# Tokens past 192 of any expert in one loop at the end of the expert part, and PLE products staged in a buffer each

## The chip, the cores and the metric

One core of a Trainium2 chip runs the kernel. The metric is the device time of one execution in microseconds; lower is better. The kernel is one layer of a trunk for 2,048 tokens of width 1,024, all in float32.

## The reference, cut to what matters

The layer has a mixer part (two token mixers, merged and added to x), an expert part, and an end part. The change touches the second and its borders:

```
h = rmsnorm(x) ; top group of 4 by softmax(h @ w_grp), then the top 2 of its 8 experts
x = x + sum over the two experts e of gate[e] * ((silu(h @ w1[e]) * (h @ w3[e])) @ w2[e])
x = x + sigmoid(rmsnorm(x) @ w_pg) * (p @ w_ple)          (PLE: p has 256 columns per token)
out = rmsnorm(x)
```

There are 32 experts with w1, w3 of 1,024 x 512 and w2 of 512 x 1,024. No expert has a limit of tokens: any of them may get from 0 to 2,048, by the data. All 4,096 assignments (two per token) have to be computed.

## The kernel before, in words

**Precision.** A float32 weight is split in two reduced-precision parts, `hi` (written by ScalarE, ACT, as a copy) and `lo` (written by VectorE, DVE, as the difference), and so are the rows. TensorE (PE) then forms three products: hi by hi, lo by hi, hi by lo. In the expert part the split weights are `ehi` (L901) and `elo` (L907), the split rows `xhi` (L882) and `xlo` (L886), and the products stand in `P` (L914).

**The order of the parts.** The mixer part takes four blocks of 512 tokens, until about 1426 us. Each block's router part gives the choice of experts; the tokens are entered in a table in DRAM, and one product counts the tokens of each expert. L803 to L813 make of the counts one integer per group of 8 experts, `codes`, with three bits per expert: over 128, over 160, over 192 tokens.

**PLE products.** `ple()` (L1019 to L1028) forms p @ w_ple for blocks 1 to 3, twelve tiles of 128 tokens by 1,024 columns: PE makes two halves (L547), ACT copies each half out of PE's accumulators into a buffer `po` (L548), and the sync engine (SP) issues its store to DRAM (L1027). The buffers of `po` carry the tag `elo` and so are the five buffers (SPL = 5) in which the `elo` splits of the expert part will live. A string, FILL, sets how the last router steps (H), the loading of expert 0's weights (E) and the PLE products (F) alternate; the products left over come after the gathers of the first two experts. Block 0's product is formed in the end part, from buffers there.

**The expert part** (L1097 to L1138) goes through the 32 experts in ORDER. For each expert SP issues twelve weight loads of 512 KB each (eight at L722, four at L729) into one of two pools, and GpSimd (POOL) gathers rows of its first 192 tokens (L841). The loads of expert 1 are made to wait for the gathered rows of expert 0 (`behind_rows`). DVE transposes the rows (`X`, L856), and then the splits and products follow a string, PART, that spells out the order of the instructions of the running expert, of the one before (its second product: T, L925, transposes; G; B, L946; Y, the copy of the results and their scatter to DRAM by POOL, L848) and of the one that follows. The first 128 tokens are computed so. Tokens 129 to 160 and 161 to 192 are computed by `some(0)` and `some(1)`, which use smaller products in plain float32.

These stand in nested branches, by the bits of the expert's code: `more` (L1129, over 128) holds `some(0)`, between whose steps GAPS puts the first products of the next expert; inside it `most` (L1131, over 160) holds `some(1)`; inside that `beyond` (L1133, over 192) holds `rest()`, a loop `For_i(192, n, 128)` with n the expert's count. Where `more` is not taken, its Else does the next expert's first products (BEGIN). Branch hints (`skip`) tell an engine ahead of time how a branch will go: for `more` on all engines, for `most` and `beyond` on PE alone. The codes are loaded in a register of each of the five engines (L1067).

**The end part** has a string of its own, FIRST, then STEPS per tile of 128 tokens: load x1 (L1153) and the two expert rows of each token (`yt`, L1155), add them by the gates (L1165), transpose (L1199), split, the product with w_pg (L1214 to L1216), sigmoid, add. The split of w_pg, `pghi` and `pglo` (L1288, L1289), is made at its start, in buffers that the expert part leaves, and block 0's PLE products (L547) are formed meanwhile.

In `ple()` a staging buffer is taken, and in the experts' code a split's buffer:

```
o = xe.tile([128, 2, 512], F32R, name="po", tag="elo", bufs=SPL)
...
xe.tile([128, 2, 512], F32R, name=name, tag=name, bufs=SPL)
```

The first instructions of expert 0 (two `hi` and `lo` splits, X, x, y) are put in order by a planner together with the PLE products ahead of them (`in_order`); what follows from L1097 on has the order that the code spells out.

Of the kernel before, what the change touches and what calls it, by code (L numbers as in the profile page):

```python
# [11 lines left out]
I32 = mybir.dt.int32  # L12
# [66 lines left out]
def tile_hybrid_block(ctx: ExitStack, tc: tile.TileContext, a, out):  # L79
# [31 lines left out]
    counts = const.tile([1, NE], I32, name="counts")  # L111
    codes = const.tile([1, NG], I32, name="codes")
# [37 lines left out]
    with ExitStack() as fin, ExitStack() as route_ctx, ExitStack() as moe_ctx:  # L150
# [148 lines left out]
        def setup_route():  # L299
# [26 lines left out]
            C["bits"] = bits = mr.tile([1, 3, NE], F32, name="bits")  # L326
            for j in range(3):
                for i in range(EPG):
                    vec.memset(bits[:, j].rearrange("o (g i) -> o g i", i=EPG)[:, :, i], float(2 ** j * 8 ** i))
# [384 lines left out]
        def load_expert(i):  # L714

            e = ORDER[i]
            w13, w2 = [], []
            for t in range(4):
                raw = r13[i % 2].tile([128, 2, 2, 512], F32, name="w13r", tag="w13")
# [86 lines left out]
        vec.tensor_copy(counts, pt[0:1, 0:NE])  # L806
        code = sm.tile([1, 3, NG], F32, name="code")
        for j, top in enumerate((128.0, 160.0, 192.0)):
            bit = C["bits"][:, j]
            vec.scalar_tensor_tensor(bit, pt[0:1, 0:NE], top, bit, op0=OP.is_gt, op1=OP.mult)  # L810
            vec.tensor_reduce(code[:, j], bit.rearrange("o (g i) -> o g i", i=EPG), axis=AX.X, op=OP.add)
        vec.tensor_tensor(code[:, 0], code[:, 0], code[:, 1], op=OP.add)
        vec.tensor_tensor(codes, code[:, 0], code[:, 2], op=OP.add)  # L813
# [44 lines left out]
        class Expert:  # L858
# [120 lines left out]
            def rest(self):  # L979

                e = self.e
                n = nc.values_load(counts[0:1, e:e + 1], min_val=0, max_val=T)
                with tc.For_i(192, n, 128) as r:
                    tv = xe.tile([128, 4], I32, name="tvd", tag="tvd", bufs=1)
                    for q in range(4):
                        pool.dma_start(
                            tv[32 * q:32 * q + 32],
                            tab_d[bass.ds(r * NE, 128 * NE)].rearrange("(q i e) o -> i e (q o)", q=4, i=32)[:, e])
                    yv = xe.tile([128, 1], I32, name="yvd", tag="yvd", bufs=1)
                    for q in range(4):  # L990
                        vec.tensor_copy(yv[32 * q:32 * q + 32], tv[32 * q:32 * q + 32, q:q + 1])
                    token_rows(vec, tv, pgrp)
                    gx = xe.tile([128, 4, 256], F32, name="gx", tag="y", bufs=2)
                    vec.memset(gx, 0.0)
                    gather(gx, tv)
                    xt = xe.tile([128, KT, 128], F32, name="xt", tag="y", bufs=2)
                    turn_rows(xt, gx)
                    ph = [mm() for _ in range(2)]
                    for k in range(KT):
                        for n in range(2):  # L1000
                            pe.matmul(ph[n], xt[:, k], self.w13[k][:, n], start=k == 0, stop=k == KT - 1)
                    t = xl.tile([128, 512], F32, name="rg", tag="yz", bufs=1)
                    act.activation(t, ph[0], AF.Silu)
                    vec.tensor_tensor(t, ph[1], t, op=OP.mult)
                    pt = px()
                    for j in range(4):
                        pe.transpose(pt[:, 128 * j:128 * j + 128], t[:, 128 * j:128 * j + 128], ident)
                    vec.tensor_copy(t, pt)
                    py = [px() for _ in range(2)]
                    for k in range(4):  # L1010
                        for c in range(2):
                            pe.matmul(py[c], t[:, 128 * k:128 * k + 128], self.w2[k][:, 512 * c:512 * c + 512],
                                      start=k == 0, stop=k == 3)
                    yr = xe.tile([128, D], F32, name="yr", tag="y", bufs=2)
                    for c in range(2):
                        act.activation(yr[:, 512 * c:512 * c + 512], py[c], AF.Copy)
                    put(yr, yv)

        def ple():  # L1019
            for m4 in range(1, NB):  # L1020
                if m4 == 3:
                    ple_turn(praw, pturn[3])
                for m in range(MB):
                    o = xe.tile([128, 2, 512], F32R, name="po", tag="elo", bufs=SPL)
                    o = o.rearrange("p n c -> p (n c)").bitcast(F32)
# [70 lines left out]

        with tc.manual_schedule():  # L1097
            ex[0].keep(())
            do(ex[0], BEGIN)
            for i in range(NE + 1):  # L1100
# [13 lines left out]
                if now is None:  # L1114
                    ple_turn(praw, pT)
# [12 lines left out]
                if now:  # L1128
                    with tc.If((code & bit) != 0, preferred_fallthrough_block=True, label=f"more{i}") as more:  # L1129
                        now.some(0, gaps(then, GAPS, f"most{i}", code, 2 * bit))  # L1130
                        with tc.If((code & 2 * bit) != 0, preferred_fallthrough_block=True, label=f"most{i}"):  # L1131
                            now.some(1, gaps(None, GAPS, f"beyond{i}", code, 4 * bit))
                            with tc.If((code & 4 * bit) != 0, preferred_fallthrough_block=True, label=f"beyond{i}"):  # L1133
                                now.rest()
                    if then:
                        then.parts = begun
                        with more.Else():
                            do(then, BEGIN)  # L1138

# [198 lines left out]
```

## Time and profile before

| | us |
|---|---|
| median of 3 runs | 2441.78 |
| lowest and highest | 2434.21, 2446.19 |
| the profiled execution: its own time | 2459.05 |
| its span | 2457.3 |
| busy: PE, DVE, ACT, POOL | 2364.7, 1440.3, 1277.6, 410.2 |
| mixer part, expert part, end part | to 1426, to about 2237, to the end |

All numbers of single instructions come from the profiled execution, whose time is 17.27 us over the median; a sum made of them is a sum against 2459.05. Times in rows are us from the span's start. PE, DVE, ACT, POOL and SP are the engines; an engine's name with a q is its sequencer, which runs branches, register operations and the issue of DMAs. "idle before <- X" tells what ended an idle time. PEclk is the granted clock of PE as a share of the full one.

### The profile page before, as it was taken

The page shows a single profiled execution, that of the slowest core. Times are in us where ns is not written, and L with a number is a line of the kernel's source. Part 1 is how long each engine was busy: PE and PEld are TensorE (multiplying, and loading weights), DVE is VectorE, ACT ScalarE, POOL GpSimd, SP SyncE. Part 2 cuts the span into 40 slices and gives each one's busy share as a digit, 9 for nine tenths or more (in the row PEclk, how much of TensorE's full clock was granted, in tenths as well). Part 3 has the DMA queues.
Part 4 walks back from the last instruction along what each step waited for, and adds up shares of the span by engine and source line. Part 5 has one row for each costly group of instructions (what it writes and reads, how often), then busy time and mean ns, then how long its engine had stood idle before and what let it go on. Part 6 is the DMA issues. An engine that isn't in the chain of part 4 may idle for free. (4 is left out here: it accounts for less than half of the span.)

```text
span 2457.3 us, 38163 instructions
## 1 busy us (share of the span) xinstructions
PE 2364.7 (96%) x13676; PEld 1898.8 (77%) x13676; DVE 1440.3 (59%) x2505; ACT 1277.6 (52%) x1963; POOL 410.2 (17%) x371
## 2 busy tenths in 40 slices
PE   7999999999999999999999998989999998998998
PEld 6888898888898978898978955666666666665887
DVE  6654445763455663536653447666666666675776
ACT  5763336752346753337733345556555655565443
POOL 1000000110000100000100033434344443431000
PEclk9999999999999999999999999999999999999999
DMA  6333443234342334442343458888779879785553
GB/s 171 92 87 95 131 138 103 65 112 129 104 150 78 87 103 129 125 126 72 100 125 98 156 177 317 308 298 321 306 294 345 308 295 343 276 340 216 196 218 125
DMA packets 313097, 445.86 MB, mean 181 GB/s; under 512 B 32442, under 2 KB 231174, under 8 KB 310752
## 3 DMA queue, kind: packets, MB, share of 16 engines
q1 hardware_dynamic: 290272, 385.68, 46.2%
q0 software_dynamic: 22528, 56.46, 6.4%
q8 instruction: 157, 2.57, 0.4%
q14 instruction: 140, 1.15, 0.1%
HBM read 401.87 MB, written 51.02 MB: 184 GB/s over the span
## 5 line engine op out<-in xcount | busy, mean ns | idle before, releaser
L182 DVE TENSOR_TENSOR wlo<-wraw,whi 128x512 fp32r<-128x512 f32 x445 | 305.1, 688 | 424.4 <-ACT whi L181 396.6
L181 ACT ACTIVATE whi<-wraw 128x512 fp32r<-128x512 f32 x448 | 281.3, 628 | 521.1 <-PE pa L206 323.9
L205 PE MATMUL pa<-h,whi 128*128 128x512 f32 x1024 | 403.4, 394 | 0.0
L206 PE MATMUL pa<-h,whi 128*128 128x512 f32 x1024 | 399.9, 390 | 0.0
L207 PE MATMUL pa<-h,wlo 128*128 128x512 f32 x1024 | 399.4, 390 | 0.0
L907 DVE TENSOR_TENSOR elo<-w13r,ehi 128x1024 fp32r<-128x1024 f32 x256 | 305.6, 1215 | 32.9 <-ACT ehi L901 12.1
L841 POOL DMA_INDIRECT rows<-h_d,tokidx x192 | 256.2, 1334 | 301.3 <-DVE elo L907 107.0
L901 ACT ACTIVATE ehi<-w13r 128x1024 fp32r<-128x1024 f32 x256 | 263.2, 1053 | 52.8 <-PE pa L914 33.4
L205 PEld LDWEIGHTS pa<-h,whi 128*128 128x128 f32 x1024 | 192.4, 188 | 42.0 <-issue 0.7
L207 PEld LDWEIGHTS pa<-h,wlo 128*128 128x128 f32 x1024 | 192.3, 188 | 40.9
L206 PEld LDWEIGHTS pa<-h,whi 128*128 128x128 f32 x1024 | 192.4, 188 | 39.5
L914 PE MATMUL pa<-ehi,xhi 128*128 128x512 f32 x512 | 182.2, 437 | 7.9 <-ACT ehi L901 3.6
L914 PE MATMUL pa<-ehi,xlo 128*128 128x512 f32 x512 | 164.2, 402 | 8.2 <-DVE xlo L886 8.2
L914 PE MATMUL pa<-elo,xhi 128*128 128x512 f32 x512 | 164.0, 402 | 0.9 <-DVE elo L907 0.8
L225 PE MATMUL pa<-whi,h 128*128 128x256 f32 x512 | 146.2, 286 | 0.1
L227 PE MATMUL pa<-whi,h 128*128 128x256 f32 x512 | 145.6, 285 | 0.0
L226 PE MATMUL pa<-wlo,h 128*128 128x256 f32 x512 | 145.3, 284 | 0.0
L226 PE MATMUL pa<-wlo,hi 128*128 128x256 f32 x512 | 143.9, 281 | 0.0
L225 PE MATMUL pa<-whi,hi 128*128 128x256 f32 x512 | 143.4, 280 | 0.0
L227 PE MATMUL pa<-whi,lo 128*128 128x256 f32 x512 | 143.3, 280 | 0.0
L914 PEld LDWEIGHTS pa<-ehi,xhi 128*128 128x128 f32 x512 | 93.2, 193 | 47.5 <-issue 29.3
L914 PEld LDWEIGHTS pa<-ehi,xlo 128*128 128x128 f32 x512 | 98.3, 192 | 31.9 <-DVE xlo L886 8.6
(319 smaller groups left out, 4525.7 us busy)
## 6 DMA issues: line engine op xcount, KB each, us to landing
w13r<-in_w_dram SPq DMA_DIRECT2D x256, 512.0 KB
wraw<-in_w_in_dram SPq DMA_DIRECT2D x320, 256.0 KB
w2r<-in_w_dram SPq DMA_DIRECT2D x128, 512.0 KB
wraw<-in_w_out_dram SPq DMA_DIRECT2D x64, 256.0 KB
yt<-y_d SPq DMA_DIRECT2D x16, 1024.0 KB
xt<-in_x_dram SPq DMA_DIRECT2D x32, 256.0 KB
wraw<-in_w_up_a_dram SPq DMA_DIRECT2D x32, 256.0 KB
wraw<-in_w_up_b_dram SPq DMA_DIRECT2D x32, 256.0 KB
```

The source lines that it names most:

```text
L181: whi = act.activation(hi, raw, AF.Copy)
L182: wlo = (pool if n < POOLG else vec).tensor_tensor(lo, raw, hi.bitcast(F32), op=OP.subtract)
L205: pe.matmul(ps, hi[:, k4], xhi, start=k == 0, stop=False)
L206: pe.matmul(ps, hi[:, k4], xlo, start=False, stop=False)
L207: pe.matmul(ps, lo[:, k4], xhi, start=False, stop=k == n_k - 1)
L225: pe.matmul(o, xhi[:, s], hi[:, k2], start=st, stop=False, skip_group_check=True)
L226: pe.matmul(o, xhi[:, s], lo[:, k2], start=False, stop=False, skip_group_check=True)
L227: pe.matmul(o, xlo[:, s], hi[:, k2], start=False, stop=k == n_k - 1, skip_group_check=True)
L841: ins = pool.indirect_dma_start(out=g[:, q], out_offset=None, in_=h2_d, in_offset=bass.IndirectOffsetOnAxis(ap=idx[:, at:at + 1], axis=0), ...
L901: act.activation(t, self.raw(k), AF.Copy)
L907: vec.tensor_tensor(t, self.raw(k), hi.bitcast(F32), op=OP.subtract)
L914: pe.matmul(self.ph[n], xp[:, k], w[:, n], start=k == 0 and w is hi and xp is self.xhi, stop=k == KT - 1 and xp is self.xlo)
```

## The change

Two things are changed.

- **PLE staging.** The twelve `po` tiles take five buffers of the tag `ehi`, then five of the tag `elo`, then two of the tag `y` (the buffers of the experts' results).
- **Tokens past 192.** The innermost branch `beyond` is taken out of every `most`, with its loop and its hint. Behind the last expert stands one branch, on a new value `beyond` (is any count over 192), and in it one loop to the largest count, `top`, that goes through all 32 experts and loads each one's weights again (12 loads, in the second pool). A hint for this branch is given on all five engines in the last round of the expert loop. The codes have two bits per expert now and their row holds `top` and `beyond` as well, each loaded in a register of each engine.

The loop's body, which the diff moves, is cut here; it uses `w13` and `w2` as loaded in place of the expert's own.

```diff
--- before.py
+++ after.py
@@ -108,8 +108,7 @@
     eps = const.tile([128, 1], F32, name="eps")
     vec.memset(eps, EPS)
     gate = const.tile([128, NT, 2], F32, name="gate")
-    counts = const.tile([1, NE], I32, name="counts")
-    codes = const.tile([1, NG], I32, name="codes")
+    codes = const.tile([1, NG + 2], I32, name="codes")
     gple = const.tile([128, KT], F32, name="gple")
     pgrp = const.tile([128, 1], F32, name="pgrp")
     plowf = const.tile([128, 1], F32, name="plowf")
@@ -323,8 +322,8 @@
             vec.memset(onesb, 1.0)
             C["acc"] = acc = mr.tile([128, NE], BF16, name="acc")
             vec.memset(acc, 0.0)
-            C["bits"] = bits = mr.tile([1, 3, NE], F32, name="bits")
-            for j in range(3):
+            C["bits"] = bits = mr.tile([1, 2, NE], F32, name="bits")
+            for j in range(2):
                 for i in range(EPG):
                     vec.memset(bits[:, j].rearrange("o (g i) -> o g i", i=EPG)[:, :, i], float(2 ** j * 8 ** i))
             pidx = sm.tile([128, 1], I32, name="pidx")
@@ -712,11 +711,13 @@
                 tc.add_manual_dep(ld.ins, ins.ins.name, SYNC, reason="the rows come first")
 
         def load_expert(i):
-
-            e = ORDER[i]
+            return load_weights(ORDER[i], r13[i % 2], i)
+
+        def load_weights(e, pl, i=0):
+
             w13, w2 = [], []
             for t in range(4):
-                raw = r13[i % 2].tile([128, 2, 2, 512], F32, name="w13r", tag="w13")
+                raw = pl.tile([128, 2, 2, 512], F32, name="w13r", tag="w13")
                 for n in range(2):
                     w = (a["w1"], a["w3"])[n][0, e].rearrange("(p k) c -> p k c", k=KT)
                     ld = nc.sync.dma_start(raw[:, n], w[:, 2 * t:2 * t + 2])
@@ -803,14 +804,16 @@
             next(last)
         pt = px()
         pe.matmul(pt[:, 0:NE], C["onesb"], C["acc"], start=True, stop=True)
-        vec.tensor_copy(counts, pt[0:1, 0:NE])
-        code = sm.tile([1, 3, NG], F32, name="code")
-        for j, top in enumerate((128.0, 160.0, 192.0)):
+        code = sm.tile([1, 2, NG], F32, name="code")
+        for j, top in enumerate((128.0, 160.0)):
             bit = C["bits"][:, j]
             vec.scalar_tensor_tensor(bit, pt[0:1, 0:NE], top, bit, op0=OP.is_gt, op1=OP.mult)
             vec.tensor_reduce(code[:, j], bit.rearrange("o (g i) -> o g i", i=EPG), axis=AX.X, op=OP.add)
-        vec.tensor_tensor(code[:, 0], code[:, 0], code[:, 1], op=OP.add)
-        vec.tensor_tensor(codes, code[:, 0], code[:, 2], op=OP.add)
+        vec.tensor_tensor(codes[:, 0:NG], code[:, 0], code[:, 1], op=OP.add)
+        top = sm.tile([1, 1], F32, name="top")
+        vec.tensor_reduce(top, pt[0:1, 0:NE], axis=AX.X, op=OP.max)
+        vec.tensor_copy(codes[:, NG:NG + 1], top)
+        vec.tensor_single_scalar(codes[:, NG + 1:NG + 2], top, 192.0, op=OP.is_gt)
         mix_ctx.close()
         xe = moe_ctx.enter_context(tc.tile_pool(name="xe", bufs=1, side="right", reuse_waits="tile"))
         rw = moe_ctx.enter_context(tc.tile_pool(name="rw", bufs=1, side="right", reuse_waits="tile"))
@@ -976,53 +979,56 @@
                 act.activation(yz, pz[:, 0:256], AF.Copy)
                 put(yz, ym[s][:, self.e:self.e + 1])
 
-            def rest(self):
-
-                e = self.e
-                n = nc.values_load(counts[0:1, e:e + 1], min_val=0, max_val=T)
-                with tc.For_i(192, n, 128) as r:
...
-                    put(yr, yv)
+        def rest(e, r):
+
+            w13, w2 = list(load_weights(e, r13[1]))[-1]
+            tv = xe.tile([128, 4], I32, name="tvd", tag="tvd", bufs=1)
...
+                    pe.matmul(ph[n], xt[:, k], w13[k][:, n], start=k == 0, stop=k == KT - 1)
...
+            put(yr, yv)
 
         def ple():
+            n = 0
             for m4 in range(1, NB):
                 if m4 == 3:
                     ple_turn(praw, pturn[3])
                 for m in range(MB):
-                    o = xe.tile([128, 2, 512], F32R, name="po", tag="elo", bufs=SPL)
-                    o = o.rearrange("p n c -> p (n c)").bitcast(F32)
+                    if n < 2 * SPL:
+                        o = xe.tile([128, 2, 512], F32R, name="po", tag=("ehi", "elo")[n // SPL], bufs=SPL)
+                        o = o.rearrange("p n c -> p (n c)").bitcast(F32)
+                    else:
+                        o = xe.tile([128, D], F32, name="po", tag="y", bufs=2)
+                    n += 1
                     ple_tile(m, pturn[m4], o)
                     nc.sync.dma_start(ple_d[m4 * MB + m], o)
                     yield
@@ -1094,6 +1100,8 @@
                     skip(label, code, bit, BUSY[:1])
                 yield
 
+        top = load(codes[0:1, NG:NG + 1], T)
+        beyond = load(codes[0:1, NG + 1:NG + 2], 1)
         with tc.manual_schedule():
             ex[0].keep(())
             do(ex[0], BEGIN)
@@ -1112,6 +1120,7 @@
                 if i + 2 < NE:
                     ex[i + 2].fetch()
                 if now is None:
+                    tc.mark_branch_hint_location("beyond", beyond, engines=QUEUED + BUSY)
                     ple_turn(praw, pT)
                 for word in PART.split():
                     if word in "nm":
@@ -1129,13 +1138,16 @@
                     with tc.If((code & bit) != 0, preferred_fallthrough_block=True, label=f"more{i}") as more:
                         now.some(0, gaps(then, GAPS, f"most{i}", code, 2 * bit))
                         with tc.If((code & 2 * bit) != 0, preferred_fallthrough_block=True, label=f"most{i}"):
-                            now.some(1, gaps(None, GAPS, f"beyond{i}", code, 4 * bit))
-                            with tc.If((code & 4 * bit) != 0, preferred_fallthrough_block=True, label=f"beyond{i}"):
-                                now.rest()
+                            now.some(1, iter(()))
                     if then:
                         then.parts = begun
                         with more.Else():
                             do(then, BEGIN)
+
+            with tc.If(beyond != 0, preferred_fallthrough_block=True, label="beyond"):
+                with tc.For_i(192, top, 128) as r:
+                    for e in range(NE):
+                        rest(e, r)
 
         moe_ctx.close()
         wg_p = fin.enter_context(tc.tile_pool(name="wg_p", bufs=1, side="right", reuse_waits="tile"))
```

## Rows read from the trace of the kernel before

**Rows 1.** Busy time by stage: us from, to, length, busy us of each engine, PEclk, DMA share, GB/s.

```profile
1473.00:1486.00 13.00, 3.22 (x9) 1.83 (x8) 5.80 (x5) 1.67 (x3) 10.26 (x10) 0.72 0.96 351
1486.00:2227.00 741.00, 696.76 (x4117) 479.51 (x4115) 496.99 (x479) 436.26 (x541) 291.55 (x226) 0.98 0.83 311
2227.00:2258.00 31.00, 24.59 (x73) 13.23 (x74) 14.23 (x14) 14.37 (x21) 4.03 (x2) 0.94 0.54 204
```

**Rows 2.** Waits of PE, 1486 to 2227: us in total, times, longest us.

```profile
PE pb L925 <- ACTq L1131: 14.4, 11, 3.4
PE pb L925 <- PEq L1131: 4.2, 2, 2.2
PE pb L925 <- ACTq L1133: 3.9, 2, 3.2
```

**Rows 3.** PE in time, 1473 to 1492: start us, us, instruction, idle before it.

```profile
1484.61 1.22 PE L914 MATMUL pa<-ehi,xlo 128*128 128x512 f32 x2 [8.15 <-DVE xlo L886]
1491.29 0.62 PE L914 MATMUL pa<-ehi,xhi 128*128 128x512 f32 x2
```

**Rows 4.** ACT in time, 1430 to 1492.

```profile
1448.09 0.60 ACT L548 ACTIVATE po<-pa 128x512 f32<-128x512 f32 x1 [1.12 <-PE pa L547]
1474.17 1.05 ACT L882 ACTIVATE xhi<-xr 128x1024 fp32r<-128x1024 f32 x1
```

**Rows 5.** DVE in time, 1461 to 1492.

```profile
1482.20 1.23 DVE L907 TENSOR_TENSOR elo<-w13r,ehi 128x1024 fp32r<-128x1024 f32 x1 [2.36 <-DMA ple_d<-po]
1483.34 1.22 DVE L886 TENSOR_TENSOR xlo<-xr,xhi 128x1024 fp32r<-128x1024 f32 x1
1484.47 1.77 DVE L856 STREAM_TRANSPOSE xr<-rows 128x1536 f32<-128x1536 f32 x1
```

**Rows 6.** Line L1027, the PLE stores: who waited for it, us, times.

```profile
  DVE elo L907: 11.1, 3
```

**Rows 7.** SP's queue in time, 1440 to 1490.

```profile
1444.50 7.97 SPq L1027 DMA_DIRECT2D ple_d<-po  x6
1459.02 5.33 SPq L1027 DMA_DIRECT2D ple_d<-po  x2
1471.92 0.33 SPq L722 DMA_DIRECT2D w13r<-in_w_dram  x1
1473.30 1.59 SPq L1027 DMA_DIRECT2D ple_d<-po  x1
```

**Rows 8.** Busy time and granted clock of stretches of 4 us, columns as in group 1.

```profile
1486.00:1490.00 4.00, 4.00 (x13) 3.14 (x12) 2.97 (x4) 2.93 (x3) 1.93 (x2) 0.64 1.01 392
1650.00:1654.00 4.00, 3.69 (x11) 3.11 (x12) 2.00 (x3) 2.66 (x4) 0.00 (x0) 0.50 0.91 315
```

**Rows 9.** Lines L1131 and L1129, the whole run: ns min/median/max, first and last start us.

```profile
L1131 PEldq COMPARE_BRANCH  x29: 71/200/2929, 1504.1 to 2210.8; - x29
L1131 POOLq INC_SWDGE_SEM  x13: 463/1046/2412, 1510.8 to 2216.4; - x13
...
L1129 PEldq COMPARE_BRANCH  x32: 75/394/6487, 1493.2 to 2222.2; - x32
```

**Rows 10.** Line L1131 from 1646.5, from 1693 and from 1882 us.

```profile
L1131 ACTq COMPARE_BRANCH  x2: 38/42/45, 1647.1 to 1650.4; - x2
...
L1131 PEldq COMPARE_BRANCH  x2: 195/1562/2929, 1693.4 to 1696.7; - x2
...
  PE pb L925: 0.7, 1
```

**Rows 11.** All engines in time, 2235 to 2254.

```profile
2237.49 0.98 POOL L848 DMA_INDIRECT y_d<-y,yi  x1 [16.19 <-ACT y L951]
...
2240.81 2.19 ACT L1288 ACTIVATE pghi<-pgraw,gple 128x1024 fp32r<-128x1024 f32 x2 [3.59 <-DMA y_d<-y,yi]
...
2253.59 0.66 PE L1199 MATMUL pb<-ident,xt 128*128 128x128 f32 x2 [4.65 <-DVE xt L1165]
```

**Rows 12.** Line L1067, the loads of the codes: ns min/median/max.

```profile
L1067 ACTq TENSOR_LOAD <-codes x4: 277/281/480, 1491.5 to 1560.1; - x4
```

More of the change, by code (lines that the diff above doesn't have):

```diff
@@ L977, in some @@
                 put(yz, ym[s][:, self.e:self.e + 1])
-            def rest(self):
-                e = self.e
-                n = nc.values_load(counts[0:1, e:e + 1], min_val=0, max_val=T)
-                with tc.For_i(192, n, 128) as r:
[L984 to L1016, printed above, removed]
-                    put(yr, yv)
@@ new lines, in rest @@
+        def rest(e, r):
+            w13, w2 = list(load_weights(e, r13[1]))[-1]
+            tv = xe.tile([128, 4], I32, name="tvd", tag="tvd", bufs=1)
+            for q in range(4):
+                pool.dma_start(
+                    tv[32 * q:32 * q + 32],
+                    tab_d[bass.ds(r * NE, 128 * NE)].rearrange("(q i e) o -> i e (q o)", q=4, i=32)[:, e])
+            yv = xe.tile([128, 1], I32, name="yvd", tag="yvd", bufs=1)
+            for q in range(4):
+                vec.tensor_copy(yv[32 * q:32 * q + 32], tv[32 * q:32 * q + 32, q:q + 1])
+            token_rows(vec, tv, pgrp)
+            gx = xe.tile([128, 4, 256], F32, name="gx", tag="y", bufs=2)
+            vec.memset(gx, 0.0)
+            gather(gx, tv)
+            xt = xe.tile([128, KT, 128], F32, name="xt", tag="y", bufs=2)
+            turn_rows(xt, gx)
+            ph = [mm() for _ in range(2)]
+            for k in range(KT):
+                for n in range(2):
+                    pe.matmul(ph[n], xt[:, k], w13[k][:, n], start=k == 0, stop=k == KT - 1)
+            t = xl.tile([128, 512], F32, name="rg", tag="yz", bufs=1)
+            act.activation(t, ph[0], AF.Silu)
+            vec.tensor_tensor(t, ph[1], t, op=OP.mult)
+            pt = px()
+            for j in range(4):
+                pe.transpose(pt[:, 128 * j:128 * j + 128], t[:, 128 * j:128 * j + 128], ident)
+            vec.tensor_copy(t, pt)
+            py = [px() for _ in range(2)]
+            for k in range(4):
+                for c in range(2):
+                    pe.matmul(py[c], t[:, 128 * k:128 * k + 128], w2[k][:, 512 * c:512 * c + 512],
+                              start=k == 0, stop=k == 3)
+            yr = xe.tile([128, D], F32, name="yr", tag="y", bufs=2)
+            for c in range(2):
+                act.activation(yr[:, 512 * c:512 * c + 512], py[c], AF.Copy)
+            put(yr, yv)
```

## Prediction

> **What bounds the kernel now.** I read the busy time by stage first [rows 1]: TensorE (PE) works 696.76 of the 741 us of the expert stage and 24.59 of the 31 us of the change-over to the end part, and 3.22 of the 13 us in which the expert stage starts. PE is the bound everywhere, so only a PE idle is worth anything: 44.2 us in the expert stage, 9.8 us at its start, 6.4 us at the change-over. The change touches all three. Then, for each of the three, I read what ended the idle.
>
> In the expert stage the waits of PE [rows 2] name L925, the transposes that follow the skip of a `most` branch: 14.4 us in 11 cases released by ACT's sequencer at L1131, 4.2 us in 2 by PE's own, 3.9 us in 2 by ACT's at L1133: 22.5 us in 15 cases, the largest single cause there.
>
> At the start the instructions of PE in time [rows 3] show 8.15 us of nothing, until `xlo` is there. `xlo` takes 1.22 us of VectorE (DVE) and needs only `xhi`, which was being written from 1474.17 for 1.05 us [rows 4]. It starts at 1483.34 [rows 5], because two `elo` splits stand ahead of it on DVE and wait for stores of PLE products, the second of them 2.36 us. Three such waits make 11.1 us [rows 6]. The sync engine (SP) issues those stores late: after two stores that end at 1464.35 it stands still for expert 0's rows until 1471.92, and one of the stores in question is issued only at 1473.30 [rows 7].
>
> **The change part by part. 1, PLE staging.** Twelve products of 1,024 columns rotate in five `elo` buffers now, so the first five `elo` splits of expert 0 meet products 7 to 11, counted from 0. Products 9, 10 and 11 are those whose stores SP issues after the standstill. With five `ehi`, five `elo` and two `y` buffers, `elo` splits 0 to 4 meet products 5 to 9. So splits 2 and 3, the two ahead of `xlo`, meet products 7 and 8, whose stores SP issued before it stood still (the pair at 1459.02 of [rows 7]). `xlo` is then ready some 1.2 us after `xhi`, at about 1476.5 in place of 1484.6. Next comes what is late next: DVE takes `xr` of expert 1 (1.77 us, at 1484.47) after `xlo` and before split 4 [rows 5], and that wants expert 1's rows, gathered behind expert 0's and landed before 1484.47. From below: rows there only at 1482.5, then 1.77 and 1.2 us to split 4, so P4 can start at 1485.4; it started at 1491.29 [rows 3], which gives 5.9. From above: the whole 8.15 us, and the clock. From 1486 to 1490 the granted clock was 0.64 [rows 8], between the two levels of 1.2 and 2.4 GHz, a loss of some 1.4 us that a shorter idle may spare, and as much before 1486. So 3 (if the rows come later still) to 11 (8.15 + 2.8); I take 8, between 5.9 and 8.15 with some of the clock.
>
> What pays for it: five `ehi` splits of expert 0 were written before the first store, when nothing held their buffers. Now they wait for the stores of products 0 to 4, which SP issues from 1444.50 [rows 7]. ScalarE (ACT) has 1.12 us idle between the 0.60 us copies of the PLE products, and a pass over 128x1024 takes 1.05 [rows 4], so five splits fit without holding up a copy. I cost this at nothing; that cover is the third rival's subject.
>
> **2, no third branch inside `most`.** No expert has over 192 tokens: the trace holds no instruction of `rest()`. `most` is tested 16 times and skipped 13 times, 29 branches at L1131 [rows 9]. A skip jumps on PE over some 112 instructions of the compiled program, on ACT over 43, which include the test for 192 and the loop. Without these, about 51 and 6 are left. The cheapest skip costs PE 0.7 us at 1882 [rows 10]. Fifteen at that price are 10.5, so 12.0 of the 22.5 us are excess, and it is not spread evenly. ACT branches at 1647.1 and again only at 1650.4, 42 ns each [rows 10], and PE waits the 3.4 us that are the longest of [rows 2]. At 1693.4 PE's own branch lasts 2.93 us [rows 10]. Nothing that the trace shows is being waited for in either, so I read both as instructions of the target that come late. A long idle is paid twice: after the one at 1647 the clock stood at 0.50 for 4 us [rows 8], half of the work of 4 us, some 2 us. Five skips show an idle of 2 to 3.4 us; at 1.7 of clock each, by the granted clock of their windows, they are worth about 8 more.
>
> Bounds: 0, if a stall does not depend on the distance, to 20 (12.0 + 8). With 6 instructions left to jump over I expect ACT's two long stalls, 3.4 and 3.2 us less the 0.7 of a plain skip, with 1.7 of clock each, to go: 8.6. PE's jump halves. The tests of `more`, which PE skips over some 185 instructions, have a median of 394 ns and a longest of 6.49 us, against 200 ns and 2.93 us for `most` [rows 9], so length seems to count, but half the length need not cure it; I take about 2.5 of PE's. Sum 11. The tests and hints for 192 themselves (three) cost PE under 1 us, and I count nothing. POOL's bookkeeping in a skip (463 to 2412 ns, 13 times) [rows 9] gets shorter, but POOL waits for ACT then, so nothing.
>
> The Trainium skill, page "Runtime: NRT & Kernel Launch", section "Instruction fetch mechanics", says that streams are fetched ahead in order and that a taken branch whose target lies outside what is held must first fetch it. The two stalls above agree with it. By that rule alone, each jump that shortens to within the held part would be free, the upper bound of 20 for this edit, while the one far jump of part 3 would stall every engine.
>
> **3, one loop at the end.** Every engine now passes one more `If`, whose body holds 32 experts' worth of code, between the last expert and the end part. The trace shows no jump of that size. From below: a short skip, 0.7 us. From above: PE's longest branch, 6.49 us [rows 9], on the path. What covers it: the last rows leave POOL at 2237.49, and ACT waits 3.59 us until 2240.81, when they have landed; the load of `yt` and the sum on DVE follow, and PE's transposes of that sum at 2253.59 end an idle of 4.65 us [rows 11]. PE meanwhile does PLE products, which can wait. So a late engine has 3 to 4 us of cover; POOL's wait and bookkeeping for the skipped gathers come after the landing and are on the path, at 0.5 to 2.4 us. A hint on all five engines stands ahead of the last expert's remaining work. I take +1.5, range 0 to +6.5.
>
> **4, small edits.** `code` is one row smaller and a maximum is taken: one small DVE operation fewer in all, far from the path. Two more values are loaded per engine at about 0.3 us (ACT's median 281 ns, longest 480 [rows 12]): SP has its 7 us standstill for it, the others issue ahead of work that queues; nothing. The body of the loop never runs.
>
> **Sum.** -8 - 11 + 1.5 = -17.5 us. The profiled execution took 2459.05 us (span 2457.3), 17.27 us or 0.7% above the median of 2441.78; by the median the sum is -17.4, so **2424**.
>
> **The rivals.** First, **only the start gains**: the code moves, and late instructions strike other skips. For it: the excess falls on a few of the 13 skips alike in shape, so place matters as well as distance. Against it: ACT jumps over 6 instructions. Price: -8 + 1.5, so 2435, no change.
>
> Second, **all the excess goes**: every jump that is left is short enough for its target to be there in time, and the start gains its most: -11 - 20 + 0.7 = -30, so 2412. The rule named above would give that in the skips. Against it: `more` still skips over some 126 instructions and `most` over 51 on PE.
>
> Third, **slower: the wait moves to ACT**. If the planner leaves the five `ehi` splits of expert 0 ahead of the PLE copies on ACT, each waits for a store (11.1/3 = 3.7 us each [rows 6], five make 18.5) with the copies behind it, and PE, whose accumulators are emptied by these copies, stops; five idles over 2 us take 1.7 of clock each, 8.5. The start then costs 18.5 + 8.5 - 8 = +19, the end 1.5, and if the skips gain nothing it is 2462. It decides as soon as PE waits for a copy between 1440 and 1460, where now the copies wait for PE [rows 4]; with the gain of part 2 in place it ends at 2451. Against it: the gaps of 1.12 us, in which a split fits.
>
> Fourth, **the change does not do what it says**: the planner keeps `xlo` behind a split that still waits (split 4 meets product 9, issued at 1472.35), or expert 1's rows are as late, and the skips are no cheaper: 0 to +1.5, so 2443.
>
> **How the numbers follow.** A measurement of this kernel can tell about 0.5%, 12.2 us, from no change, so faster is under 2429.6 and slower over 2454.0. Chances: the forecast 0.42 (its own range 2417 to 2435, from 5.9 to 10 at the start, 5 to 15 in the skips, 0 to 4 at the end; 0.35 of it under 2429.6); only the start 0.22 (0.05 under the bound); all excess 0.11; the slower one 0.12, of which 0.08 over 2454.0; no effect 0.13. Faster 0.51, no change 0.41, slower 0.08. The range that holds 8 in 10 goes from 2410, past the second rival, to 2444, which takes in the first and the fourth.
>
> **What would show it.** Right: in the waits of DVE at L907 on PLE stores nearly nothing; `xlo` before 1478 on this profile's scale and PE's idle at the start under 4 us; PE at L925 behind L1131 in sum 12 us or less, ACT's sequencer never over 2 us; the time from the last put to PE's first transposes of the end part at most 2 us longer than the 16.1 us of before. Wrong: PE idle between the PLE products, a wait on expert 1's rows as long as the old one, stalls at L925 of 3 us elsewhere, or an end part that starts 5 us later.

## The result, and the profile after

The changed kernel took 2414.84 us (median of 4 runs, 2413.47 to 2416.54) beside 2439.9 for the kernel before (4 runs, 2434.21 to 2446.19): ratio 0.9897, interval 0.9878 to 0.9915, so 25 us or 1.0% less. Forecast were 2424 and 17.4 us less; 2414.84 lies below the forecast's own range (2417 to 2435), inside the wide one (2410 to 2444), and nearest to the second rival's 2412. The profiled execution of before lay 19 us above its median and that of after on it (2414.01), so the 44.9 us between the two spans (2457.3 and 2412.4) overstate the change; below, medians give the sizes and the traces only tell where.

The stages of after, as in [rows 1] (the expert stage here ends at 2182):

```profile
1473.00:1486.00 13.00, 6.75 (x26) 4.73 (x26) 4.31 (x4) 2.92 (x5) 10.31 (x9) 0.97 1.00 387
1486.00:2182.00 696.00, 670.50 (x4097) 469.76 (x4097) 499.18 (x479) 437.95 (x540) 284.92 (x225) 0.99 0.87 330
2182.00:2213.00 31.00, 24.69 (x73) 13.14 (x74) 13.93 (x13) 14.37 (x21) 4.60 (x2) 0.94 0.53 201
```

PE's idle in the expert stage is 25.5 us where it was 44.2. But PE's busy time is 26 us less as well. Some 5 of these are the 20 matmuls that now fall ahead of 1486 (4097 of 4117 are left, at a mean near 0.23 us); for the other 21 the forecast had only the clock. The change-over is what it was.

PE's waits from 1440 to 2230, the answer to [rows 2] (line numbers are 3 higher or more; L1138 is the test of `more`, L1140 that of `most`, L1147 the new branch at the end), and behind them one wait of before:

```profile
PE pb L928 <- ACTq L1140: 10.0, 13, 2.7
PE pb L928 <- DVE elo L910: 8.7, 15, 3.9
PE pa L917 <- DVE elo L910: 6.3, 1, 6.3
...
PE pa L546 <- ACTq L1147: 0.9, 1, 0.9
```

```profile
PE pb L925 <- DVE elo L907: 3.7, 2, 3.4
```

The 22.5 us behind skips have become 10.0: twelve idles of 0.57 to 0.70 us and one of 2.73. But the waits of the same transposes for DVE's `elo` splits grew from 3.7 to 8.7 us, with two of 2.54 and 3.92 among them, and a wait of 6.3 us at the start is new. The one of 3.92 leads to ACT, whose split DVE waits for:

```profile
1972.83 2.00 ACT L904 ACTIVATE ehi<-w13r 128x1024 fp32r<-128x1024 f32 x2 [3.71 <-issue]
L904 ACTq EVENT_SEMAPHORE  x4: 17/28/38, 1972.6 to 1972.8; - x4
```

ACT's branch of `more` stands at 1968.6 and its next instructions, checks of semaphores of at most 38 ns, only at 1972.6. So ACT was held by nothing that it checks: its instructions came late, now behind `more`, where its jump is shorter too.

PE and DVE at the start, the answer to [rows 3, 5] (P0 to P7 are the eight groups of six split products that an expert's first 128 tokens take; P4 is the first that needs split 4):

```profile
1475.75 0.74 PE L917 MATMUL pa<-ehi,xlo 128*128 128x512 f32 x2 [0.84 <-DVE xlo L889]
1487.36 1.22 PE L917 MATMUL pa<-elo,xhi 128*128 128x512 f32 x2 [6.32 <-DVE elo L910]
```

```profile
1474.47 1.22 DVE L889 TENSOR_TENSOR xlo<-xr,xhi 128x1024 fp32r<-128x1024 f32 x1
1484.38 1.78 DVE L859 STREAM_TRANSPOSE xr<-rows 128x1536 f32<-128x1536 f32 x1 [8.69 <-DMA rows<-h_d,tokidx]
1486.08 3.49 DVE L910 TENSOR_TENSOR elo<-w13r,ehi 128x1024 fp32r<-128x1024 f32 x3
```

`xlo` starts at 1474.47 in place of 1483.34 and PE's 8.15 us are down to 0.84, as forecast. Then DVE stands 8.69 us before expert 1's rows with split 4 behind it, and PE loses 6.32 us at P4. PE's two idles make 7.16 us where there was one of 8.15.

The branches, the answer to [rows 9], and behind them the queues that bring instructions, first of before, then of after (packets, MB, share):

```profile
L1140 PEldq COMPARE_BRANCH  x32: 71/198/2062, 1501.9 to 2164.6; - x32
L1138 PEldq COMPARE_BRANCH  x32: 66/447/2332, 1492.0 to 2175.8; - x32
```

```profile
q8 instruction: 157, 2.57, 0.4%
q14 instruction: 140, 1.15, 0.1%
```

```profile
q8 instruction: 149, 2.44, 0.4%
q14 instruction: 93, 0.76, 0.1%
```

PE's longest branch fell from 2.93 to 2.06 us for `most` and from 6.49 to 2.33 us for `more`, and a third fewer packets of instructions came by the second queue. The program is also shorter now, so the packets alone do not show that jumps became cheaper.

### The profile page after: what moved, and what is told of

Its sections match the earlier page's. It is cut to its first block, busy times and chain, and to the rows that moved or that the text cites. A ratio compares the mean times of both kernels' runs of the same rounds, so it can differ in the third digit from the quotient of the medians.

```text
span 2412.4 us, 37864 instructions
## 1 busy us (share of the span) xinstructions
PE 2341.8 (97%) x13676; PEld 1891.0 (78%) x13676; DVE 1442.0 (60%) x2496; ACT 1279.5 (53%) x1963; POOL 405.3 (17%) x371
## 4 chain that ended last, share of the span: by engine, by line
PE 65%; DMA 21%; issue 8%; POOL 3%; DVE 3%; ACT 1%; POOLq 0%; SPq 0%; ACTq 0%; DVEq 0%
DMA rows<-h_d,tokidx 19%; PE pa L204 12%; PE pa L205 12%; PE pa L206 12%; PE pa L224 5%; PE pa L225 5%; PE pa L226 5%; PE pa L1228 2%; PE pa L1227 2%; PE pa L1226 2%; POOL rows L844 2%; DMA y_d<-yz,ym 2%; PE pb L460 1%; POOL y_d L851 1%; PE pb L445 1%
## 5 line engine op out<-in xcount | busy, mean ns | idle before, releaser
L844 POOL DMA_INDIRECT rows<-h_d,tokidx x192 | 243.2, 1267 | 85.6 <-issue 53.2
L917 PEld LDWEIGHTS pa<-elo,xhi 128*128 128x128 f32 x512 | 96.7, 189 | 27.6 <-DVE elo L910 6.7
```

The source lines that it names most:

```text
L844: ins = pool.indirect_dma_start(out=g[:, q], out_offset=None, in_=h2_d, in_offset=bass.IndirectOffsetOnAxis(ap=idx[:, at:at + 1], axis=0), ...
L917: pe.matmul(self.ph[n], xp[:, k], w[:, n], start=k == 0 and w is hi and xp is self.xhi, stop=k == KT - 1 and xp is self.xlo)
```

## The experiments

The kernels ran on three chips, A, B and C below. The kernel before differs much from chip to chip (medians 2455.21, 2439.69 and 2456.82), so a ratio is to before on the same chip.

| run | median us | ratio to before, interval |
|---|---|---|
| stage_only (A) | 2454.15 | 0.9992, 0.9976 to 1.0009 |
| loop_only (A) | 2411.66 | 0.9827, 0.9803 to 0.9851 |
| no_end_if (A) | 2416.27 | 0.9842, 0.9819 to 0.9865 |
| x1_late (A) | 2406.9 | 0.9805, 0.9782 to 0.9829 |
| short_third (B) | 2441.8 | 1.0011, 1.0002 to 1.0019 |
| straight_body (B) | 2429.52 | 0.9962, 0.995 to 0.9973 |
| x1_nostage (B) | 2414.76 | 0.9905, 0.9891 to 0.992 |
| changed_again (B) | 2412.78 | 0.9894, 0.9881 to 0.9908 |
| before_shift (C) | 2459.65 | 1.0008, 0.9993 to 1.0024 |
| shift128 (C) | 2423.28 | 0.9871, 0.9851 to 0.9891 |
| short_third_at (C) | 2424.33 | 0.9872, 0.9851 to 0.9893 |
| no_end_at (C) | 2415.07 | 0.9834, 0.9814 to 0.9853 |

### The two halves of the change

The first run takes the new `ple()` into the kernel before, the second the old one into the changed kernel, which turns this diff round.

```diff
-                    o = xe.tile([128, 2, 512], F32R, name="po", tag="elo", bufs=SPL)
-                    o = o.rearrange("p n c -> p (n c)").bitcast(F32)
+                    if n < 2 * SPL:
+                        o = xe.tile([128, 2, 512], F32R, name="po", tag=("ehi", "elo")[n // SPL], bufs=SPL)
...
```

> The kernel before with the PLE staging alone changed. Theory: the start gains what the two traces show there. Expert 0's second product of P4 began at 1491.75 before and at 1487.36 after, 4.4 us earlier, 1.8 of them by an earlier start of the first product; so about 2435.5 (ratio to before 0.998, 0.996 to 1.000). Rival: the staging is the larger part of the 25 us, by the clock that stays up and by what follows: 2420 or less (0.992). Second rival: an unchanged expert part hides it all: 2440.

> The changed kernel with the PLE products staged as before, so only the loop past 192 is moved. Theory: this is the larger part, about -20 us: 2420 (ratio 0.992, 0.990 to 0.994), with PE idle at L928 behind the skip of most near 0.6 us in nearly every case. Rival: without the staging the late instructions only strike elsewhere: 2433 or more (0.997).

The staging alone gives nothing that can be measured (0.9992), and the loop alone gives 1.7% on this chip, 43.5 us where 20 were expected. The kernel before was some 15 us slower on this chip than on B and in the first comparison. Without staging the changed kernel is even not slower: 2411.66, beside 2412.78 and 2414.84 with it on other chips. So staging as it stands is neutral: changed_again's 2412.78 lies between the two cases that its expectation (below) told apart. Both expectations above had the right order, but the staging's 4.4 us were not there. PE in stage_only, then in loop_only:

```profile
1474.75 1.22 PE L914 MATMUL pa<-ehi,xlo 128*128 128x512 f32 x2 [0.83 <-DVE xlo L886]
1486.40 1.22 PE L914 MATMUL pa<-elo,xhi 128*128 128x512 f32 x2 [4.72 <-issue]
1492.66 0.63 PE L914 MATMUL pa<-ehi,xhi 128*128 128x512 f32 x2
```

```profile
1481.47 1.22 PE L917 MATMUL pa<-ehi,xlo 128*128 128x512 f32 x2 [8.02 <-issue]
1492.23 0.62 PE L917 MATMUL pa<-ehi,xhi 128*128 128x512 f32 x2
```

The last row of each is the first pair of products of P7, and expert 0's first pair began at 1472.46 and 1472.26. With staging PE has two idles and is slow twice: a pair of products takes 1.05 us or more behind each of them in place of 0.62, because the granted clock falls. In the changed kernel the 4 us around the second idle's end read:

```profile
1486.00:1490.00 4.00, 2.64 (x6) 2.16 (x7) 4.00 (x5) 3.81 (x5) 1.01 (x1) 0.50 1.02 385
```

That is the lower of the two levels, 1.2 GHz. Without staging it has one idle, and by P7 the two kernels, counted from their first products, stand 0.2 us apart (20.20 and 19.97 us).

### What follows at the start

```diff
+PART0 = "n h3 l3 P2 h4 l4 P3 h5 l5 P4 h6 l6 h7 l7 v0 u0 m P5 v1 u1 P6 X x y H0 L0 P7 H1 L1 S"
-                for word in PART.split():
+                for word in (PART0 if i == 0 else PART).split():
```

X, x and y are the transposed rows of the next expert and their two splits, which stand behind P6 now.

> The changed kernel with the transposed rows and splits of expert 1 put behind expert 0's second weight splits, in the first round only. It tests whether the 6.32 us that PE waits at 1487.36 is the wait for expert 1's rows on DVE ahead of split 4. Theory: yes, so the 6.3 us go, and with them some 2 to 3 us of low clock: 2406 (ratio to before 0.986). Rival: the next thing is as late (the rows themselves, or the weights of expert 1 behind them on the sync engine), and the time stays within 2 us of the changed kernel's 2414.8.

> The kernel with the loop moved, PLE products staged as before, and expert 1's rows put later as in the run with them late. Theory: expert 0's low rows still come 8 us late, because two splits ahead of them wait for stores, and the clock drops once; so as with the loop moved alone, 2411 to 2412 (ratio to before 0.983), while staging and late rows together gave 2407. Rival: the order of expert 1's rows is enough by itself: 2407 or less.

With expert 1's rows behind the weight splits the changed kernel takes 2406.9, the lowest of all kernels here: 0.9805 to before and 4.8 us less than loop_only on the same chip, and 6 to 8 less than the changed kernel had on two others. It beats both kernels compared. The wait of 6.3 us is gone; PE in x1_late has only this at that place, and DVE finds the rows there:

```profile
1474.98 1.22 PE L918 MATMUL pa<-ehi,xlo 128*128 128x512 f32 x2 [0.19 <-DVE xlo L890]
```

```profile
1484.49 1.78 DVE L860 STREAM_TRANSPOSE xr<-rows 128x1536 f32<-128x1536 f32 x1
```

Without the staging the same order gives 2414.76, some 3 us more than expected and no better than the changed kernel beside it (2412.78): `xlo` waits for the stores and nothing is won. So the two need each other: the staging moves the wait from `xlo` to expert 1's rows, and only with both moved is it gone.

### The branch at the end

```diff
-            with tc.If(beyond != 0, preferred_fallthrough_block=True, label="beyond"):
-                with tc.For_i(192, top, 128) as r:
...
-                        rest(e, r)
```

> The changed kernel without the branch behind the last expert, its hint and the loads of its two values (leaves out tokens past 192 of an expert, of which these inputs have none). It prices the one far jump. Theory: little, since the last rows' landing covers it: 0.9 us of PE idle and 0.4 us later transposes in the trace, so 1 to 2 us less than the changed kernel: 2413 (ratio to before 0.989). Rival: the jump holds all engines and POOL's wait for the landing is on the path: 5 us or more less, 2409 (0.987).

The second run also keeps two small tiles of the loop and the size of a third, so that all others lie where they did:

```diff
+                    elif now:
+                        for n, name in ((4, "tvd"), (1, "yvd")):
+                            pool.memset(xe.tile([128, n], I32, name=name, tag=name, bufs=1), 0)
```

> The changed kernel without the branch behind the last expert, with its tiles at the changed kernel's addresses (leaves out tokens past 192). The run without it and with other addresses had 229 to 232 ns per product and 2416. Theory: 227 ns, and the branch at the end costs 1 to 3 us, so 2411 to 2413. Rival: 2414 to 2416, the branch costs nothing and the code before it is delivered less well.

no_end_if took 2416.27 and no_end_at, at the changed kernel's addresses, 2415.07, so without the branch the kernel is no faster than with it (2412.78 to 2414.84): the far jump costs nothing that shows, as the second run's rival had it. In after:

```profile
2191.88 0.97 POOL L851 DMA_INDIRECT y_d<-y,yi  x1 [16.86 <-ACTq L1147]
...
2195.58 2.19 ACT L1300 ACTIVATE pghi<-pgraw,gple 128x1024 fp32r<-128x1024 f32 x2 [3.98 <-DMA y_d<-y,yi]
```

The last rows land as late behind their scatter as before (3.98 us of waiting, 3.59 in [rows 11]). PE's first transposes of the end part come at 2208.57, 16.7 us after the last scatter where it was 16.1.

### Length, loop, or the third branch

```diff
-                                now.rest()
+                                vec.memset(spare, 0.0)
```

> The kernel before with the third branch, its tests and hints kept, and its body (the loop) cut to one small VectorE operation (leaves out tokens past 192 of an expert, of which these inputs have none). Theory: what costs is the length of code that a skip jumps over, so this is nearly as fast as the kernel with the loop moved: ratio to before 0.983 to 0.988. Rival: what costs is the third level of test, hint and join itself: 0.996 or more.

The second run takes the loop out and was meant to keep the length:

```diff
-                with tc.For_i(192, n, 128) as r:
+                for r in (192,):
```

> The kernel before with the body of the third branch as straight code, one pass over tokens 193 to 320, without the loop and the load of its count (leaves out tokens past 320, of which there are none). Nearly the same length of code, no loop. Theory (length): no or little gain, ratio to before 0.994 to 1.001. Rival: the loop itself costs (its register load, the counter and the semaphores of a loop): 0.99 or less.

The first (1.0011) missed its theory and fell in its rival's range. The second (0.9962) lies in its theory's range, though its 10 us are well clear of the noise. Neither is the clean test that it was meant to be.

straight_body did not keep the length. A large part of the old body was the loop's own code: without it the jump over `most` falls in the compiled program from 112 to 85 instructions on PE and from 43 to 18 on ACT, and the packets of the second instruction queue from 140 to 104, where after has 93:

```profile
q14 instruction: 104, 0.85, 0.1%
```

So it does not separate the loop from the length. In short_third the waits behind ACT at the skip are short, none over 0.7 us (nor is one in straight_body), but those for DVE's `elo` are long:

```profile
PE pb L926 <- DVE elo L908: 14.7, 7, 4.8
PE pb L926 <- ACTq L1132: 8.1, 13, 0.7
```

Three of them, of 4.04, 4.83 and 4.83 us, make most of the 14.7. What was gained behind ACT was lost there, and some 3 us more in the products themselves (234 ns each in place of 232 to 233).

### The place in on-chip memory

What was read is the distance between the starts of pairs of split-weight products, in a stretch without waits. In before, after, shift128 and before_shift, first and last pair of such a stretch:

```profile
1820.12 0.64 PE L914 MATMUL pa<-ehi,xhi 128*128 128x512 f32 x2
...
1824.31 0.63 PE L914 MATMUL pa<-ehi,xhi 128*128 128x512 f32 x2
```

```profile
1783.70 0.62 PE L917 MATMUL pa<-ehi,xhi 128*128 128x512 f32 x2
...
1788.24 0.61 PE L917 MATMUL pa<-elo,xhi 128*128 128x512 f32 x2
```

```profile
1784.97 0.63 PE L919 MATMUL pa<-ehi,xhi 128*128 128x512 f32 x2
...
1789.62 0.62 PE L919 MATMUL pa<-elo,xhi 128*128 128x512 f32 x2
```

```profile
1850.37 0.62 PE L914 MATMUL pa<-ehi,xhi 128*128 128x512 f32 x2
...
1853.09 0.62 PE L914 MATMUL pa<-ehi,xhi 128*128 128x512 f32 x2
```

In before it is 4.19 us for 9 pairs, 233 ns per product; in after 4.54 for 10, 227 ns. The change takes `counts` (128 bytes) out of the constants, and with it the split rows `xhi` move from byte 30752 to 30624 of a partition, and with them the other tiles of their pool (`xlo` and the second product's `ghi` and `glo` among them). Two runs change nothing but this: one puts an unused constant of that size into the changed kernel, one gives `counts` a scratch tile in the kernel before.

```diff
+    counts = const.tile([1, NE], I32, name="counts")
+    vec.memset(counts, 0)
```

```diff
-    counts = const.tile([1, NE], I32, name="counts")
+    counts = junk[0:1, 0:2 * NE].bitcast(I32)
```

> The changed kernel with an unused constant of 128 bytes, so that the expert part's tiles lie as in the run with the staging alone (xhi at 30752). Theory (address): 232 ns per product and 9 to 10 us more than the changed kernel, 2423 to 2425. Rival: 227 ns and 2413 to 2415.

> The kernel before, with the 128 bytes of counts put into a scratch tile, so that everything of the expert part lies in on-chip memory (SBUF) where the kernel with the loop moved has it: the split rows xhi at 30624 in place of 30752 bytes of a partition, the split weights where they were. Nothing else changes. In the traces so far the distance between the starts of two split-weight products is 232 ns in all kernels with xhi at 30752 and 227 ns in all with 30624. Theory (address): 227 ns, and some 1,900 products by 5 ns make 9 us less, ratio to before 0.996. Rival (the rate comes from the code of the branches, not the address): 232 ns and 1.000.

> The changed kernel once more, beside the others on one chip. Expected 2413.5 to 2416.5; then staging costs 2 to 4 us against the kernel with the loop moved alone (2411.7), and the end branch's removal (2416.3) gives nothing. If it is 2412 or less, the staging is neutral and the differences between these kernels are those of runs and chips.

The rate follows the place in both directions: 4.65 us for 10 pairs (233 ns) in shift128, 2.72 for 6 (227 ns) in before_shift. shift128 takes 2423.28, 8.4 and 10.5 us more than the changed kernel on two other chips (2414.84 and 2412.78): 1,920 products (60 per expert) by 5 ns are 9.6. Against no_end_at on the same chip (2415.07, 227 ns) it is 8.2 us. But before_shift takes no less than before (1.0008). There PE's four largest waits, for the whole expert stage, are these:

```profile
PE pb L925 <- ACTq L1131: 12.0, 10, 3.6
PE pb L966 <- DVE sg L964: 11.7, 7, 3.0
PE pb L925 <- PEq L1131: 6.3, 3, 2.2
PE pb L925 <- DVE elo L907: 6.0, 9, 4.3
```

They make 36.0 us, and the same four 26.7 in the trace of before (14.4, 4.4, 4.2 and 3.7): by these two traces, what the products gain is lost in waits. The two traces were not taken side by side, so why the waits grow stays open.

Last, the short body laid out at the changed kernel's addresses, without `counts` and with two small tiles as the body:

```diff
-                                now.rest()
+                                for n, name in ((4, "tvd"), (1, "yvd")):
+                                    vec.memset(xe.tile([128, n], I32, name=name, tag=name, bufs=1), 0)
```

> The kernel before with the third branch kept and its body cut to two small operations, laid out in SBUF exactly as the kernel with the loop moved (leaves out tokens past 192). The run before with such a body had 234 ns per product. Theory (address and late instructions, each by itself): 227 ns, 13 us less than that run, 2428 (ratio to before 0.995); what then remains over the kernel with the loop moved is late instructions on VectorE. Rival (the third level of test and join costs by itself): 2438 or more at 227 ns.

It takes 2424.33, 0.9872, near its theory, in place of 1.0011 for the same branches at other addresses. short_third had `xhi` at 30784 and 234 ns, which by 1,920 products makes some 13 of the 17.5 us between the two; they ran on different chips.

Chip C has the cleanest comparison of all. before_shift and short_third_at have the same branches, the same places and the same rate, and differ in the body alone: 2459.65 and 2424.33, so the body of the third branch, which never runs, costs 35.3 us there. What is left against no_end_at on that chip, without the third branch (and with the staging, which was neutral), is 9.3 us; against loop_only (2411.66 on chip A), with the same place and the same rate, 12.7. On chip B the short body of short_third won nothing, so how much it is worth depends on the chip, on the place or on both; no run tells them apart. PE's waits behind the skip, short_third_at first, then loop_only:

```profile
PE pb L923 <- DVE elo L905: 10.9, 5, 5.3
PE pb L923 <- ACTq L1129: 8.3, 13, 0.8
```

```profile
PE pb L928 <- ACTq L1135: 10.0, 13, 2.7
PE pb L928 <- DVE elo L910: 2.9, 3, 2.6
```

and one of those 5 us on DVE in short_third_at:

```profile
1826.59 0.68 DVE L918 TENSOR_TENSOR g<-pa,g 128x512 f32<-128x512 f32 x1
1832.33 1.23 DVE L905 TENSOR_TENSOR elo<-w13r,ehi 128x1024 fp32r<-128x1024 f32 x1 [5.06 <-DMA w2r<-in_w_dram]
L905 DVEq EVENT_SEMAPHORE  x2: 21/35/49, 1832.2 to 1832.2; - x2
```

DVE's branch of `more` stands at 1826.2 and its next instructions, two checks of semaphores, at 1832.2. They last 49 ns at most, so no semaphore held DVE there. The load that the profile names is no operand of this split, and ACT had read the same weights at 1826.22; so these are instructions that came late, now on DVE. The same checks last 50 ns at most at all three long waits of short_third. What made them late is not shown.

## Why the prediction was right, and where it was not

The time lies in the wide range, 9 us below the number and below the forecast's own range. That it is not farther off is in part luck: the start gave 0 in place of 8 us and the skips more than their 11, and what came out larger did so partly for a reason that was not in the sum, the rate of the products.

**PLE staging, forecast -8, measured 0 (0.9992).** Three things came as forecast: the waits of `elo` on stores went, `xlo` was done at 1475.7 (forecast 1476.5), and ACT's five splits found their place among the copies (1448.94 to 1455.83). The first of them waited 1.68 us for a store and delayed a copy (at 1449.91, 3.25 us behind the one before, where 1.72 is usual), which the forecast had excluded, but PE went on without a stop.

The step that failed is the bound of what is late next: expert 1's rows were taken for there at 1482.5, and DVE got them at 1484.38, beyond that bound. Split 4 thus came when it did before, 1486.08 and 1486.17, in a kernel whose expert stage began 1.8 us earlier, and PE's idle fell by 1.0 us (8.15 to 7.16), where the sum had 5.9 from below and 3 should the rows come later still. A second error lies in the clock: I let a shorter idle spare some of it, but two idles replace one, and it fell behind both. x1_late shows both in the other direction: with expert 1's rows out of the way, staging and new order together are worth 4.8 us against loop_only on one chip.

**The skips, forecast -11, in range 0 to -20; loop_only gave 43.5 us on its chip, the whole change 27 and 25 on two others.** By shift128 some 8 to 10 us of this are the products' rate; the sum had no such term, and no row of before showed that 232 ns was not the best. With 9 taken off, 16 to 18 are left (34 on chip A), which I put down to the late instructions that I had meant. That is a subtraction and not a measurement: in the kernel before the same better rate won nothing. The traces bear it out in part. Behind the skip, waits of 22.5 us became 10.0, a plain one 0.58 in place of 0.7, so nearly all of the excess of 12.0 went, as the second rival had it; but the waits for DVE's `elo` at the same place rose by 5.0 (one of them, of 3.92, by a late ACT), for which I had no term.

That length counts, my reason for ACT and PE, is borne out in part. For it: in straight_body, short_third and short_third_at, where ACT jumps over 18 or 8 instructions at `most` in place of 43, none of the waits for its sequencer is over 0.8 us, and on chip C the short body alone is worth 35.3 us. Against it: after, with 5, still has one of 2.73 there and ACT late by some 4 us behind `more`; DVE is late with the short body, by up to 5 us; and short_third won nothing. So I had the kind of stall right and was wrong in expecting ACT's long ones to go; which engine is struck, and where, length alone does not tell, and that stays open.

The Trainium skill, page "Runtime: NRT & Kernel Launch", section "Instruction fetch mechanics", says that a taken branch out of what is held forces a fetch. The fewer packets of the instruction queues (93 for 140) fit that, but would follow from a shorter program as well. That each shorter jump would then be free, as I read out of the Trainium skill there, short_third does not show: its packets (91 on that queue) are as few, and its waits for DVE are larger (14.7 us for 3.7).

**The end, forecast +1.5, measured 0 to 0.6.** The cover held: the landing of the last rows hides it. By the same section of the Trainium skill, as the prediction read it, the far jump would hold every engine; whether it held PE cannot be told, since PE had work queued until 2190.98 and lost 0.93 us.

**The rivals.** The first, that only the start gains, fell the other way round: only the skips gained. Its mechanism, late instructions that strike elsewhere, did occur: in after on ACT behind `more`, in short_third and short_third_at on DVE. The second, that all the excess goes, is nearest in time and in the skips, but not by its mechanism alone: its start did not gain, and the rate was in no rival. The slower one, ACT stopped by its splits, did not occur. Of the fourth, half occurred: expert 1's rows were as late.

**The signs.** As named for right: the waits on stores gone, `xlo` before 1478, 10.0 us at L928, an end part 0.6 us later. Against them: PE's idle at the start is 7.16 us and not under 4, ACT's sequencer is over 2 us once (2.7), and two signs of being wrong came, DVE's wait for expert 1's rows (8.69 us) and a wait of over 3 us at L928 behind another branch (3.92; before had one of 3.41 there).

## What to carry to other kernels

Before a wait is removed, look for the instruction that stands next on the same engine and price its own wait from the latest landing that the trace allows, and count a clock loss for each idle that remains. A kernel with code that is jumped over can pay on any engine that gets its next instructions late, so the number of long waits per engine is to be read after each change of the code, not only at the line that was shortened. A run that is to hold the length and vary something else must have its jumps counted first, and one that is to vary the code must hold the tiles in place. Where busy time changes with the same instructions, compare the distance between neighbouring ones: here tiles that moved by 128 bytes were the reason.

## What the runs showed of the hardware that was not expected

A split-weight product of 128x512 took 227 ns from start to start with `xhi` at byte 30624 of a partition and 232 to 233 with it at 30752; with `xhi` at 30784 and the split weights 64 bytes higher it was 234, and with `xhi` at 30624 and the weights 64 bytes higher, in no_end_if, 229 to 232 (so 30624 alone does not give 227 ns, as the expectation of before_shift had it). The plain float32 products of the same shape took the same in all that were compared (eight in 3.59 to 3.60 us). Which accesses meet there was not tried. And the time of the kernel before depends on its chip (medians from 2439.7 to 2456.8), while those with the loop moved differ little (2407 to 2416 on all chips, 2423 with the shift).
